# Cached memory keys of a decoder step: turned in 32x32 squares on VectorE in place of whole transposes on TensorE

## The chip, the cores and the metric

The kernel runs on one core of a Trainium2 chip. The metric is the device time of one execution in microseconds: the median of three timed runs is 949.08, between 947.50 and 950.35. A profile of one execution stands beside them. All numbers are in float32 at the inputs and outputs.

## The reference, cut to what matters

The program is one layer of a decoder for two groups with the same weights: a prompt of 512 rows and a sample group of 8 sequences with 4 new rows each. The layer has a mixer (an mLSTM and a differential attention), a cross-attention into 256 memory tokens, and a gated feed-forward with a short convolution. The change touches the cross-attention of the sample group alone:

```python
# h: (8, 4, 1024) normalised rows; cache_mem_k, cache_mem_v: (8, 256 tokens, 4 heads, 256)
q = (h @ w_mq).reshape(B, T, 4, 256)
s = einsum('bqhd,bkhd->bhqk', q, mk) * 256 ** -0.5
p = softmax(s, axis=-1)
o = einsum('bhqk,bkhd->bqhd', p, mv).reshape(B, T, 1024)
return o @ w_mo
```

Each of the 8 sequences has its own keys and values, 1 MB of each, which no other sequence shares: 8.4 MB of keys and 8.4 MB of values are read for 32 query rows.

## The kernel before, in words

Matmuls contract over the 128 partitions, so the scores need keys with the feature on the partition, and memory holds them with the token there. Products with weights split each operand into a rounded part and a rest (three matmuls per product); products of the sample rows are plain float32 matmuls with 32 columns of weights, put on the four 32-column groups of the array in turn. Such a plain float32 product stands in the trace as two records, a transpose or a product of rounded parts as one.

A planner orders the instructions of every engine when the program is built, by the place in the program, raised priorities (`tc.high_priority`) and a simulated clock; each engine then runs its list strictly in that order. `burst(t)` makes an instruction follow `t` at once. A tile is taken from a pool with a fixed number of buffers and waits until the buffer's last user has finished.

The stage around the change runs like this.

1. The query projection `gemmB(hqT, [ev_q(m) ...])`: eight column tiles of w_mq, of which m = 0 to 3 come first and m = 4 to 7 in a loop of 16 steps. `ev_q` scales each result; the sample rows' part goes to `qs` (feature on the partition, 32 query rows).
2. `mk_load(i)` reads one of 16 key tiles (sequence b, token half c): 128 tokens on the partitions, 4 KB each, into one of six `stage` buffers. `mk_turn(i)` makes eight 128x128 transposes on TensorE, and ScalarE and VectorE copy the results out of PSUM into a `kT` tile (one of the four weight slots, one tile for each sequence). Tiles 0 to 7 are turned inside the projection's loop, 8 to 15 between the first and the second four sequences' scores.
3. `mk_scores(b)`: eight products of 256 columns for each sequence (4 heads x 2 feature halves). All 32 query rows are multiplied with the keys of one sequence, and only this sequence's four rows count. `sample_exp` takes maximum and exponential for each sequence.
4. `sample_softmax` (shared with the decode attention of the mixer) mixes the eight sequences' rows through `csz` into one tile of 128 rows (sequence, head, row) x 256 tokens, which is transposed twice and spread into `az`.
5. `mv_load` and `mv_out` do the value products: `VORD` is their order, the first six tiles in stage buffers, the others in the four weight slots and one large buffer.

Between these, `next(prompt)` puts one step of the prompt group's cross-attention (scores, softmax, transposes, value products, in a pipeline four deep) into TensorE's stream. All loads of this stage are issued on SP's queue in order, with the weights of w_mo behind them.

Of the kernel before, what the change touches and what calls it, by code (L numbers as in the profile page):

```python
# [32 lines left out]
CONST_COLS = {}  # L33
_off = 0
for _n, _w in (("ident", 128), ("cos", 40), ("sin", 40), ("nsin", 40), ("dmask", 8), ("cm4", 4), ("cA", 1), ("cB", 1),
               ("comb", 16), ("selD", 8), ("selX", 8), ("selB", 8), ("cmask", 128), ("maskT", 128), ("maskS", 32)):
    CONST_COLS[_n] = (_off, _w)
    _off += _w
CONST_W = _off
# [38 lines left out]
def kernel(ctx: ExitStack, tc: tile.TileContext, I, O):  # L78
# [23 lines left out]
    def S(shape, dt, name):  # L102
        return sp.tile(list(shape), dt, name=name, tag="S")
# [10 lines left out]
    def at(name="at"):  # L114
        return psa.tile([P, 512], F32, name=name, tag="at")
# [11 lines left out]
    def v2(t, b):  # L127
        return t.rearrange("p (a b) -> p a b", b=b)
# [26 lines left out]
    def con(n, p=P):  # L155
        o, w = CONST_COLS[n]
        return cpk[:p, o:o + w]
# [51 lines left out]
    def stage():  # L209
        return stg.tile([P, 1024], F32, name="wst", tag="st")  # L210
# [847 lines left out]
    def sample_softmax(sall, su, coef, sel, oname, between=None):  # L1058


        cf = small(NB, "scf")
        nc.vector.reciprocal(out=cf, in_=su)
        if coef is not None:
            VTS(out=cf, in0=cf, scalar1=coef, scalar2=None, op0=MUL)
        VTT(out=cf, in0=cf, in1=sel, op=MUL)
        VTT(out=view(csz, 0, [(64, NB // 2), (48, 2), (1, 16)]),
            in0=con("comb").unsqueeze(1).unsqueeze(1).broadcast_to([P, NB // 2, 2, 16]),
            in1=cf.rearrange("p (i e) -> p i e", e=2).unsqueeze(3).broadcast_to([P, NB // 2, 2, 16]), op=MUL)
        az = S([P, 2, H, NB * NS], F32, oname + "z")
        nc.gpsimd.memset(az, 0.0)  # L1070
# [7 lines left out]
        behind = between() if between else None  # L1078
        pT = at("spt")
# [7 lines left out]
        return a, [az[:, 0], az[:, 1]]  # L1087

    def gather(name, b, g, out):
        v = nc.sync.value_load(ptab[0:1, 2 * b + g:2 * b + g + 1], min_val=0, max_val=I[name].shape[1] - 1)  # L1090
# [303 lines left out]
        split(mvN[0][:, c], mvN[1][:, c], st)  # L1394

    qs = sm.tile([P, 8, NS], F32, name="qs", tag="qz", bufs=1)
    qh, ql = [], []

    def ev_q(m):
        if m % 2 == 0:  # L1400
            qh.append(npool.tile([P, 2, 516], F32R, name="qh", tag="N"))
        if m % 4 == 0:
            ql.append(S([P, 4, SEQ], F32R, "ql"))

        def ev(i, c0, c1, ps):
            n = min(c1, SEQ) - c0
            q = qh[m // 2][:, m % 2, c0:c0 + n]
            nc.scalar.mul(out=q, in_=ps[:, :n], mul=1.0 / 16.0)
            STT(out=ql[m // 4][:, m % 4, c0:c0 + n], in0=ps[:, :n], scalar=1.0 / 16.0, in1=f32(q), op0=MUL, op1=SUB)
            if i == 1:  # L1410
                nc.scalar.mul(out=qs[:, m, :], in_=ps[:, n:n + NS], mul=1.0 / 16.0)
        return ev

    run(gemmB(hqT, [ev_q(m) for m in range(4)], half_first=True))
# [44 lines left out]
            j = 2 * (h % 2) + e  # L1459
            put(oT, h // 2, j, j + 1, 0, SEQ, po.unsqueeze(1))  # L1460

    kst, kts, vts = {}, {}, {}

    def mk_load(i):
        b, c = i // 2, i % 2
        kst[i] = stage()
        dma(out=kst[i], in_=I["cache_mem_k"][0, b, c * P:(c + 1) * P].rearrange("t h d -> t (h d)"))

    def mk_turn(i):
        b, c = i // 2, i % 2  # L1470
        if c == 0:
            kts[b] = wp.tile([P, 8, 256], F32, name="kT", tag="W")
        for q in range(2):
            ps = at("tpk")
            for j in range(4):
                t = tr(ps[:, j * P:(j + 1) * P], kst[i][:, (4 * q + j) * P:(4 * q + j + 1) * P], ident)
            (VCP if q else nc.scalar.copy)(out=kts[b][:, 4 * q:4 * q + 4, c * P:(c + 1) * P], in_=v2(ps, P))
        return t.ins

    def mk_scores(b):  # L1480
        ps = mmp("ssc")[:, :256]
        for c in range(2):
            for h in range(H):
                t = mm(ps[NS * h:NS * h + NS], lhsT=qs[:, 2 * h + c], rhs=kts[b][:, 2 * h + c, :], start=(c == 0), stop=(c == 1))
        sample_exp(sall, b, ps, nm, su)
        return t.ins

    def mv_load(b):

        if 2 < b:  # L1490
            t = wp.tile([P, 2, DM], F32, name="vt", tag="W") if b < 7 else S([P, 2, DM], F32, "vt")
            vts[b] = [t[:, 0], t[:, 1]]
        else:
            vts[b] = [stage(), stage()]
        for c in range(2):
            dma(out=vts[b][c], in_=I["cache_mem_v"][0, b, c * P:(c + 1) * P].rearrange("t h d -> t (h d)"))

    VORD = [(b, 1 - c if b in (2, 7) else c) for b in (2, 1, 0, 7, 6, 5, 4, 3) for c in range(2)]

    def mv_out(bs):  # L1500

# [7 lines left out]
    sall = S([P, NB, 256], F32, "cas")  # L1509
    nm, su = small(NB, "snm"), small(NB, "ssu")  # L1510
    prompt = pipe(8, ch_soft, lambda i: None, ch_turn, ch_out)

    for i in range(6):
        mk_load(i)
    for i, _ in enumerate(gemmB(hqT, [ev_q(m) for m in range(4, 8)])):
        if i % 4 == 3:
            for j in (i // 2 - 1, i // 2):
                mk_turn(j)
                mk_load(j + 6)

    next(prompt)
    for b in range(4):
        t = mk_scores(b)
    with tc.issue_after(t):
        for j in range(8, 16):
            t = mk_turn(j)
            if j + 6 < 2 * NB:
                mk_load(j + 6)
            if j == 11:
                next(prompt)  # L1530
    for b in range(3):
        mv_load(b)
    next(prompt)
    with tc.issue_after(t):
        for b in range(4, NB):
            t = mk_scores(b)
    for b in range(3, NB):
        mv_load(b)
    next(prompt)
    with tc.high_priority():  # L1540
        _, az = sample_softmax(sall, su, None, con("selX"), "ca")
    for _ in range(NMID):
        next(prompt, None)
    pso = mmp("pso")[:, :256]
# [347 lines left out]
def _constants():  # L1892
# [28 lines left out]
    put("selD", ((r % 16 // TS)[:, None] == np.arange(NB)[None, :] % 4).astype(np.float32))  # L1921
    put("selB", ((r // 16)[:, None] == np.arange(NB)[None, :]).astype(np.float32))
    put("selX", ((r % NS // TS)[:, None] == np.arange(NB)[None, :]).astype(np.float32))
    return {"consts": c}


# [20 lines left out]
```

## Time and profile before

| | |
|---|---|
| timed runs, median (lowest to highest) | 949.08 us (947.50 to 950.35) |
| the profiled execution, first to last instruction | 947.0 us, its own time; no other is given for it |
| TensorE busy | 927.3 us, 98% of the span |
| VectorE, ScalarE, GpSimd busy | 601.1, 388.5, 195.9 us |
| bytes moved | 130.27 MB, mean 138 GB/s |
| TensorE's granted clock, mean | 0.995 |

TensorE's matmuls are pipelined: a record begins before the one ahead has ended, so a sum of durations counts overlap twice. What a group costs in the stream is the time from its first start to the start of what follows. PE is the matmul side of TensorE, PEld its weight loads, DVE is VectorE, ACT ScalarE, POOL GpSimd and SP the queue that issues DMAs (SPq in the rows).

### The profile page before, as it was taken

Reading aid. Unit: us, or ns where it says so; the run is one execution under the profiler, and the core shown is the slowest. Engines: PE = TensorE matmul, PEld = TensorE weight load, DVE = VectorE, ACT = ScalarE, POOL = GpSimd, SP = SyncE. Lnnn points to the kernel's source line nnn. Section 1 sums busy time; section 2 is a strip of 40 time slices with the busy share of each in tenths; the row PEclk is TensorE's granted clock in tenths of the full one; section 3 lists DMA queues with packets and bytes.
Section 4 is the critical chain, followed back from the end, with each engine's and each line's share of the span. In section 5 each row is a group of like instructions: output and inputs, shape, how many; then the busy total and the mean of one; then the engine's idle time right before and its main releaser. Section 6 shows DMA issues by size and latency. Waiting matters only on the chain. (4 is left out here: it accounts for less than half of the span.)

```text
span 947.0 us, 17080 instructions
## 1 busy us (share of the span) xinstructions
PE 927.3 (98%) x6612; PEld 808.2 (85%) x6612; DVE 601.1 (63%) x1128; ACT 388.5 (41%) x750; POOL 195.9 (21%) x384
## 2 busy tenths in 40 slices
PE   8999999999999999999999999999999999999995
PEld 5899787889866778998777899989988998999974
DVE  6745145565887448735654778637757775676767
ACT  5655233344676457625544433322212222222232
POOL 6611000025432215300000554001110110110114
PEclk9999999999999999999999999999999999999998
DMA  8960023344870429946944732062043313512023
GB/s 273 301 197 7 1 89 137 89 123 139 270 265 7 165 97 340 297 155 211 358 167 135 209 122 80 26 179 67 17 133 108 94 27 96 149 49 90 24 92 117
DMA packets 120673, 130.27 MB, mean 138 GB/s; under 512 B 8567, under 2 KB 86232, under 8 KB 120592
## 3 DMA queue, kind: packets, MB, share of 16 engines
q1 hardware_dynamic: 114408, 125.69, 42.1%
q10 hardware_dynamic: 6184, 3.48, 1.2%
q8 instruction: 52, 0.85, 0.4%
q14 instruction: 29, 0.24, 0.1%
HBM read 112.22 MB, written 16.93 MB: 136 GB/s over the span
## 5 line engine op out<-in xcount | busy, mean ns | idle before, releaser
L485 PE MATMUL mm<-fT,wslot 128*128 128x256 f32 x1872 | 235.9, 288 | 0.0
L485 PEld LDWEIGHTS mm<-fT,wslot 128*128 128x128 f32 x1872 | 234.4, 188 | 1.8 <-issue 0.8
L146 ACT CAST wslot<-wst 128x1024 fp32r<-128x1024 f32 x125 | 130.8, 1050 | 251.3 <-issue 71.7
L147 DVE TENSOR_TENSOR wslot<-wst,wslot 128x1024 fp32r<-128x1024 f32 x125 | 155.1, 1245 | 81.3 <-ACT wslot L146 80.8
L1758 PE MATMUL mm<-wslot,act 128*128 128x512 f32 (+1 forms) x180 | 70.2, 391 | 0.0
L1759 PE MATMUL mm<-wslot,act 128*128 128x512 f32 (+1 forms) x180 | 70.0, 392 | 0.0
L1757 PE MATMUL mm<-wslot,act 128*128 128x512 f32 (+1 forms) x180 | 69.3, 387 | 0.0
L1663 POOL COPY cvo<-u 128x2 f32<-128x2 f32 x43 | 10.5, 243 | 203.6 <-DVE u L1661 193.5
L411 PE MATMUL mm<-wslot,hT 128*128 128x512 f32 x128 | 51.3, 402 | 0.0
L485 PE MATMUL mm<-hT,wslot 128*128 128x256 f32 (+1 forms) x384 | 51.0, 289 | 0.0
L413 PE MATMUL mm<-wslot,hT 128*128 128x512 f32 x128 | 51.0, 399 | 0.0
L412 PE MATMUL mm<-wslot,hT 128*128 128x512 f32 x128 | 50.8, 397 | 0.0
L1658 DVE TENSOR_TENSOR u<-mm,rsb 128x256 f32<-128x256 f32 x43 | 18.1, 424 | 50.0 <-PE mm L485 50.0
L485 PEld LDWEIGHTS mm<-hT,wslot 128*128 128x128 f32 x384 | 49.2, 188 | 0.5 <-issue 0.2
L1757 PEld LDWEIGHTS mm<-wslot,act 128*128 128x128 f32 x180 | 34.3, 191 | 8.0 <-issue 0.8
L1759 PEld LDWEIGHTS mm<-wslot,act 128*128 128x128 f32 x180 | 33.8, 188 | 7.3 <-issue 0.4
L1758 PEld LDWEIGHTS mm<-wslot,act 128*128 128x128 f32 x180 | 33.8, 188 | 7.2
L1675 ACT ACTIVATE c<-c 128x560 f32<-128x560 f32 x21 | 14.1, 672 | 56.7 <-DVE c L1669 56.7
L1669 DVE SCALAR_TENSOR_TENSOR c<-u,cvT,c 128x560 f32<-128x560 f32 x43 | 34.3, 797 | 0.9
L1668 DVE SCALAR_TENSOR_TENSOR c<-u,cvT,c 128x560 f32<-128x560 f32 x43 | 34.1, 793 | 0.2
L1770 DVE TENSOR_TENSOR yp<-mm,yp 128x512 f32<-128x512 f32 (+1 forms) x41 | 27.2, 673 | 5.2 <-PE mm L1759 5.1
L413 PEld LDWEIGHTS mm<-wslot,hT 128*128 128x128 f32 x128 | 24.1, 188 | 5.0
(476 smaller groups left out, 1850.8 us busy)
## 6 DMA issues: line engine op xcount, KB each, us to landing
wst<-in_w_up_dram SPq DMA_DIRECT2D x42, 512.0 KB
wst<-in_w_in_dram SPq DMA_DIRECT2D x28, 512.0 KB
wst<-in_w_down_dram SPq DMA_DIRECT2D x20, 512.0 KB
wst<-in_cache_mem_k_dram SPq DMA_DIRECT2D x16, 512.0 KB
vt<-in_cache_mem_v_dram SPq DMA_DIRECT2D x10, 512.0 KB
wst<-in_w_mk_dram SPq DMA_DIRECT2D x8, 512.0 KB
xb<-in_x_prompt_dram SPq DMA_DIRECT2D x8, 512.0 KB
wst<-in_cache_dk_dram SPq DMA_DIRECT2D x16, 256.0 KB
```

Of the source, the lines that this page charges most:

```text
L146: nc.scalar.copy(out=hi, in_=src)
L147: (eng or nc.vector).tensor_tensor(out=lo, in0=src, in1=f32(hi), op=SUB)
L411: mm(ps[b], lhsT=xt.hi(k, c0, c0 + n), rhs=s[:, 0, kk, :], start=(k == 0), stop=False)
L412: mm(ps[b], lhsT=xt.hi(k, c0, c0 + n), rhs=s[:, 1, kk, :], start=False, stop=False)
L413: return mm(ps[b], lhsT=xt.lo(k, c0, c0 + n), rhs=s[:, 0, kk, :], start=False, stop=(k == nk - 1))
L485: mm(ps[i], lhsT=s[:, l, k, :], rhs=x(k, c0, c1), start=(k == 0 and j == 0), stop=(k == 7 and j == 2))
L1668: STT(out=c, in0=u[:, 1:EXT - 1], scalar=w[1], in1=c, op0=MUL, op1=ADD)
L1669: STT(out=c, in0=u[:, 0:EXT - 2], scalar=w[0], in1=c, op0=MUL, op1=ADD)
L1757: mm(ps, lhsT=t[:, 0, c0:c0 + P], rhs=s[:, 0, i % 2, cs], start=st, stop=False)
L1758: mm(ps, lhsT=t[:, 0, c0:c0 + P], rhs=s[:, 1, i % 2, cs], start=False, stop=False)
L1759: return mm(ps, lhsT=t[:, 1, c0:c0 + P], rhs=s[:, 0, i % 2, cs], start=False, stop=en)
L1770: VTT(out=y, in0=ps, in1=y, op=ADD)
```

## The change

The keys of all four heads of 32 tokens are read by one DMA for each head: head h goes to partitions 32h to 32h+31, with the token within 32 on the partition and four blocks of 32 tokens behind each other. `nc.vector.transpose` then turns every 32x32 square of the tile in place, so that partition 32h + f holds feature f of head h for a block of 32 features. The queries lie in `qx`, zero but for a block-diagonal: row 32h + f of block j, and one column for each sequence, head and row. One product then contracts 32 features of all four heads at once, for a pair of sequences' 32 query columns; eight blocks of features fall on four column groups, twice each. `mk_sum` adds the four groups and picks a sequence's 16 columns by a matrix of zeros and ones (`selE`), which gives the tile of 128 rows directly, and one softmax works on it. Keys and values of a sequence use the same buffers (`two`, `home`), and the order of sequences is 0, 2, 4, 6, 1, 3, 5, 7. `attend_T` is the end of `sample_softmax`, taken out; the decode attention still uses both.

```diff
+    qx = cst.tile([P, 8, NB, 4 * TS], F32, name="qx", tag="xs")
+    nc.gpsimd.memset(qx, 0.0)
+    def mq_spread(h):
+        for j in range(4):
+            nc.gpsimd.tensor_copy(out=view(qx[NS * h:NS * h + NS, j, :, TS * h:TS * h + TS], 0, [(512, 2), (16, NB), (1, TS)]),
+                                  in_=qs[NS * j:NS * j + NS, 2 * h:2 * h + 2, :].rearrange("p c (n t) -> p c n t", t=TS))
...
                 nc.scalar.mul(out=qs[:, m, :], in_=ps[:, n:n + NS], mul=1.0 / 16.0)
+                if m % 2 == 1:
+                    mq_spread(m // 2)
...
+    SEQS, HOMES = (0, 2, 4, 6, 1, 3, 5, 7), (0, 1, 2, 7, 3, 4, 5, 6)
+    home = dict(zip(SEQS, HOMES))
+    def two(i):
+        if i < 3:
+            return [stage(), stage()]
+        t = wp.tile([P, 2, DM], F32, name="kvt", tag="W") if i < 7 else S([P, 2, DM], F32, "kvt")
+        return [t[:, 0], t[:, 1]]
+    def mk_load(b):
+        kst[b] = two(home[b])
         for c in range(2):
             for h in range(H):
-                t = mm(ps[NS * h:NS * h + NS], lhsT=qs[:, 2 * h + c], rhs=kts[b][:, 2 * h + c, :], start=(c == 0), stop=(c == 1))
-        sample_exp(sall, b, ps, nm, su)
+                dma(out=v2(kst[b][c][NS * h:NS * h + NS], 256),
+                    in_=I["cache_mem_k"][0, b, c * P:(c + 1) * P, h].rearrange("(k t) d -> t k d", t=NS))
+    def mk_turn(b):
+        for t in kst[b]:
+            nc.vector.transpose(out=t, in_=t)
+    def mk_scores(bs):
+        t = None
+        for b in bs:
+            ps = mmp("ssc")[:, :256]
+            for c in range(2):
+                kv = kst[b][c].rearrange("p (k j t) -> p k j t", j=8, t=NS)
+                for j in range(8):
+                    g = NS * (j % 4)
+                    with burst(t):
+                        t = mm(v2(ps[g:g + NS, c * P:c * P + P], NS), lhsT=qx[:, j, b // 2 * 2:b // 2 * 2 + 2].rearrange("p n r -> p (n r)"),
+                               rhs=kv[:, :, j, :], start=(j < 4), stop=(j >= 4)).ins
+            nc.scalar.copy(out=sc[:, b], in_=ps)
+        return t
+    def mk_sum(last):
+        t = None
+        for b in SEQS:
+            i = NS * (b // 2)
+            with tc.issue_after(last) if t is None else burst(t):
+                t = mm(pS[i:i + NS], lhsT=con("selE")[:, NS * (b % 2):NS * (b % 2) + NS], rhs=sc[:, b], start=(b % 2 == 0),
+                       stop=(b % 2 == 1)).ins
+    def mem_softmax():
+        nm, su = small(NB, "snm")[:, 0:1], small(NB, "ssu")[:, 0:1]
+        VRED(out=nm, in_=pS, axis=AX.X, op=MAX, negate=True)
+        a = Z("spc")[:, :256]
+        ACT(out=a, in_=pS, func=AF.Exp, bias=nm, accum_out=su)
+        nc.vector.reciprocal(out=su, in_=su)
+        VTS(out=a, in0=a, scalar1=su, scalar2=None, op0=MUL)
+        return attend_T(a, "ca")
...
-    VORD = [(b, 1 - c if b in (2, 7) else c) for b in (2, 1, 0, 7, 6, 5, 4, 3) for c in range(2)]
+    VORD = [(SEQS[k], 1 - c if k in (2, 3) else c) for k in (2, 1, 0, 3, 7, 6, 5, 4) for c in range(2)]
...
+    pS = at("pS")[:, :256]
+    for k in range(4):
+        mk_load(SEQS[k])
     for i, _ in enumerate(gemmB(hqT, [ev_q(m) for m in range(4, 8)])):
+        if i % 4 == 1:
+            mk_turn(SEQS[i // 4])
         if i % 4 == 3:
-            for j in (i // 2 - 1, i // 2):
-                mk_turn(j)
-                mk_load(j + 6)
+            mk_load(SEQS[4 + i // 4])
     next(prompt)
...
     next(prompt)
+    sc = S([P, NB, 256], F32, "sc")
+    mk_scores(SEQS[:4])
+    for k in range(3):
+        mv_load(SEQS[k])
+    mv_load(SEQS[3])
+    for k in range(4, 8):
+        mk_turn(SEQS[k])
     next(prompt)
+    t = mk_scores(SEQS[4:])
+    for k in range(4, 8):
+        mv_load(SEQS[k])
+    next(prompt)
+    mk_sum(t)
     with tc.high_priority():
-        _, az = sample_softmax(sall, su, None, con("selX"), "ca")
+        az = mem_softmax()
```

## Rows read from the trace of the kernel before

**Rows 1.** The page's first lines: busy us (share of the span) and records

```profile
span 947.0 us, 17080 instructions
PE 927.3 (98%) x6612; PEld 808.2 (85%) x6612; DVE 601.1 (63%) x1128; ACT 388.5 (41%) x750; POOL 195.9 (21%) x384
```

**Rows 2.** Windows: length, then busy PE, PEld, DVE, ACT, POOL, clock, DMA share, GB/s

```profile
404.00:436.00 32.00, 32.00 (x265) 32.00 (x264) 9.50 (x19) 9.34 (x24) 1.81 (x1) 1.00 0.46 144
436.00:456.00 20.00, 19.94 (x233) 15.44 (x231) 13.37 (x30) 11.43 (x36) 0.00 (x0) 1.00 0.85 291
...
450.00:470.00 20.00, 19.94 (x186) 15.86 (x185) 13.83 (x36) 12.38 (x44) 0.00 (x0) 1.00 1.02 393
```

**Rows 3.** TensorE's timeline, cross-attention stage: start us, length us, line, operation, count

```profile
414.39 0.60 PE L1476 MATMUL tpk<-cpk,wst 128*128 128x128 f32 x4
414.74 4.00 PE L485 MATMUL mm<-hqT,wslot 128*128 128x256 f32 x30
...
434.10 1.47 PE L1476 MATMUL tpk<-cpk,wst 128*128 128x128 f32 x12
435.32 0.48 PE L1427 MATMUL sca<-mkT,qh 128*128 128x256 f32 x2
...
436.92 1.05 PE L1484 MATMUL ssc<-kT,qs 128*32 128x256 f32 x10
437.90 0.66 PE L1476 MATMUL tpk<-cpk,wst 128*128 128x128 f32 x4
438.49 3.22 PE L1484 MATMUL ssc<-kT,qs 128*32 128x256 f32 x54
441.64 1.53 PE L1476 MATMUL tpk<-cpk,wst 128*128 128x128 f32 x12
442.93 0.48 PE L1427 MATMUL sca<-mkT,qh 128*128 128x256 f32 x2
...
447.61 5.09 PE L1476 MATMUL tpk<-cpk,wst 128*128 128x128 f32 x40
452.63 3.66 PE L1484 MATMUL ssc<-kT,qs 128*32 128x256 f32 x64
...
470.48 2.80 PE L1506 MATMUL pso<-wst,caz 128*32 128x256 f32 x48
...
475.55 4.52 PE L1506 MATMUL pso<-vt,caz 128*32 128x256 f32 x80
```

**Rows 4.** TensorE's timeline: value products of the decode attention, and the softmax mixing

```profile
286.57 1.95 PE L1337 MATMUL ops<-vt,daz 128*32 128x128 f32 x64
288.46 0.94 PE L1281 MATMUL oda<-dvN,aT 128*128 128x128 f32 x6
...
460.52 1.07 PE L1075 MATMUL spa<-cas,csz 128*32 128x256 f32 x16
```

**Rows 5.** Groups by line on VectorE, 404 to 486: count, busy us, mean ns, idle before

```profile
L1477 DVE COPY kT<-tpk 128x512 f32<-128x512 f32 x16 | 11.0, 686 | 9.0 <-PE tpk L1476 9.0
```

**Rows 6.** Instructions by tile, whole trace: count, ns least/median/most, first and last start

```profile
L318 DVE TENSOR_SCALAR hN<-xb,rs x5: 731/753/756, 22.0 to 48.2; 128x1024 f32<-128x1024 f32 x4, 32x1024 f32<-32x1024 f32 x1
...
L147 DVE TENSOR_TENSOR wslot<-wst,wslot x125: 1187/1220/2319, 31.4 to 916.3; 128x1024 fp32r<-128x1024 f32 x125
...
L1221 POOL COPY kT<-dkT x8: 191/198/199, 222.3 to 260.8; 128x16 f32<-128x16 f32 x8
...
L254 SPq DMA_DIRECT2D wst<-in_w_up_dram x44: 367/378/1684, 512.0 to 853.2; - x44
...
L1141 SPq DMA_DIRECT2D xb<-in_x_sample_dram x1: 337/337/337, 289.8 to 289.8; - x1
```

**Rows 7.** Timeline of SP's queue, waits between issues included: start us, length us

```profile
393.36 29.74 SPq L1467 DMA_DIRECT2D wst<-in_cache_mem_k_dram  x10
```

**Rows 8.** Bytes moved from 290.5 to 292.5, in 40 columns of 0.05 us

```profile
GB/s 0 0 0 0 0 328 410 328 246 328 246 82 0 0 0 246 328 82 0 0 0 0 0 0 0 0 0 0 0 0 0 0 0 0 0 0 0 0 0 0
```

More of the change, by code (lines that the diff above doesn't have):

```diff
@@ L35 @@
 for _n, _w in (("ident", 128), ("cos", 40), ("sin", 40), ("nsin", 40), ("dmask", 8), ("cm4", 4), ("cA", 1), ("cB", 1),
-               ("comb", 16), ("selD", 8), ("selX", 8), ("selB", 8), ("cmask", 128), ("maskT", 128), ("maskS", 32)):
+               ("comb", 16), ("selD", 8), ("selX", 8), ("selB", 8), ("selE", 64), ("cmask", 128), ("maskT", 128), ("maskS", 32)):
     CONST_COLS[_n] = (_off, _w)
@@ L1068, in sample_softmax @@
             in1=cf.rearrange("p (i e) -> p i e", e=2).unsqueeze(3).broadcast_to([P, NB // 2, 2, 16]), op=MUL)
-        az = S([P, 2, H, NB * NS], F32, oname + "z")
-        nc.gpsimd.memset(az, 0.0)
         w = sall.shape[2]
@@ L1078, in sample_softmax, with attend_T @@
         behind = between() if between else None
+        return a, attend_T(a, oname, behind)
+    def attend_T(a, oname, behind=None):
+        az = S([P, 2, H, NB * NS], F32, oname + "z")
+        nc.gpsimd.memset(az, 0.0)
         pT = at("spt")
@@ L1086, in sample_softmax @@
                 nc.scalar.copy(out=view(az, g * 1024 + h * 256, [(36, NB), (1, TS)]), in_=src[:, h])
-        return a, [az[:, 0], az[:, 1]]
+        return [az[:, 0], az[:, 1]]
     def gather(name, b, g, out):
@@ L1460, in ch_out @@
             put(oT, h // 2, j, j + 1, 0, SEQ, po.unsqueeze(1))
[L1462 to L1478, printed above, removed]
@@ L1480, in mk_scores @@
-    def mk_scores(b):
-        ps = mmp("ssc")[:, :256]
+    kst, vts = {}, {}
+    SEQS, HOMES = (0, 2, 4, 6, 1, 3, 5, 7), (0, 1, 2, 7, 3, 4, 5, 6)
[7 more added lines that the diff above has]
+        kst[b] = two(home[b])
         for c in range(2):
             for h in range(H):
-                t = mm(ps[NS * h:NS * h + NS], lhsT=qs[:, 2 * h + c], rhs=kts[b][:, 2 * h + c, :], start=(c == 0), stop=(c == 1))
-        sample_exp(sall, b, ps, nm, su)
-        return t.ins
@@ L1488, in mv_load @@
-    def mv_load(b):
[L1490 to L1494, printed above, removed]
+                dma(out=v2(kst[b][c][NS * h:NS * h + NS], 256),
[3 more added lines that the diff above has]
+            nc.vector.transpose(out=t, in_=t)
@@ L1495, in mv_load @@
+    def mv_load(b):
+        vts[b] = two(home[b])
         for c in range(2):
             dma(out=vts[b][c], in_=I["cache_mem_v"][0, b, c * P:(c + 1) * P].rearrange("t h d -> t (h d)"))
-    VORD = [(b, 1 - c if b in (2, 7) else c) for b in (2, 1, 0, 7, 6, 5, 4, 3) for c in range(2)]
+    VORD = [(SEQS[k], 1 - c if k in (2, 3) else c) for k in (2, 1, 0, 3, 7, 6, 5, 4) for c in range(2)]
     def mv_out(bs):
@@ L1507, in mv_out @@
                            rhs=vts[b][c][:, 256 * h:256 * h + 256], start=((b, c) == VORD[0]), stop=((b, c) == VORD[-1])).ins
-    sall = S([P, NB, 256], F32, "cas")
-    nm, su = small(NB, "snm"), small(NB, "ssu")
     prompt = pipe(8, ch_soft, lambda i: None, ch_turn, ch_out)
-    for i in range(6):
-        mk_load(i)
+    pS = at("pS")[:, :256]
+    for k in range(4):
+        mk_load(SEQS[k])
     for i, _ in enumerate(gemmB(hqT, [ev_q(m) for m in range(4, 8)])):
+        if i % 4 == 1:
+            mk_turn(SEQS[i // 4])
         if i % 4 == 3:
-            for j in (i // 2 - 1, i // 2):
-                mk_turn(j)
-                mk_load(j + 6)
+            mk_load(SEQS[4 + i // 4])
     next(prompt)
[L1522 to L1532, printed above, removed]
-    next(prompt)
[L1534 to L1538, printed above, removed]
-    next(prompt)
+    next(prompt)
+    sc = S([P, NB, 256], F32, "sc")
[5 more added lines that the diff above has]
+        mk_turn(SEQS[k])
+    next(prompt)
+    t = mk_scores(SEQS[4:])
[3 more added lines that the diff above has]
+    mk_sum(t)
     with tc.high_priority():
-        _, az = sample_softmax(sall, su, None, con("selX"), "ca")
+        az = mem_softmax()
     for _ in range(NMID):
@@ L1923, in _constants @@
     put("selX", ((r % NS // TS)[:, None] == np.arange(NB)[None, :]).astype(np.float32))
+    put("selE", np.concatenate([((r % NS)[:, None] == s[None, :]) & (s[None, :] // 16 == e) for e in range(2)], 1))
     return {"consts": c}
```

## The prediction

> **What bounds the kernel now.** I read the page's first lines, then the windows by stage, then TensorE's timeline of the stage that the change touches. TensorE is busy for 98% of the span [rows 1]; in the cross-attention stage it is busy 32.00 of 32 us and 19.94 of 20 us, at a granted clock of 1.00 (the 2.4 GHz level), while VectorE, ScalarE and GpSimd have half of their time free or more [rows 2]. So an instruction that leaves TensorE's stream gives back its own time, as long as the rest of the stream still finds its data. The other engines and the transfers matter only as possible new waits. The timeline is read from start to next start, since matmul ends overlap.
>
> **Turning squares leaves TensorE: -14.0 us.** The 128 transposes of `mk_turn` stand in twelve groups between matmuls. A group of 12 lasts 1.22 to 1.29 us (434.10 to 435.32, 441.64 to 442.93), and there are five; a group of 4 lasts 0.35 (414.39 to 414.74), once 0.59 (437.90 to 438.49), and there are five; one of 40 lasts 5.02 (447.61 to 452.63); one of 8 lies between and is taken at the same 0.1 us each [rows 3]. Sum: 5 x 1.24 + 4 x 0.35 + 0.59 + 0.8 + 5.0 = 14.0 us. All lie on TensorE's unbroken stream.
>
> **Scores: 0 (from -0.2 to +7.7).** Before, 64 products of 256 columns run as 128 records: 0.98 us for 10 (436.92 to 437.90), 3.15 for 54 (438.49 to 441.64) and 3.66 for 64, 7.7 us in all [rows 3]. After, 8 sequences x 2 tiles x 8 blocks = 128 products of 128 columns on four 32-column groups in turn, 256 records. The decode attention's value product has this very shape: 64 records from 286.57 to 288.46, 29.5 ns each [rows 4]. 256 x 29.5 ns = 7.6 us. What differs is that the moving operand now comes in four runs of 32 elements; no row shows that, and I bound it by the old pace per record (57 ns, +7.7 for 256 records started at half the columns) and take the nearest row, so 0. Each sequence is multiplied by a pair's 32 query columns, half of them unused, which costs no more than the 32-column shape of that row.
>
> **Selector sums: 0.** `mk_sum` is 8 products of 32x256, as the eight that mix `csz` in before: 16 records, 1.07 us [rows 4]. They change places.
>
> **Softmax: off the path, 0.** Eight maxima on VectorE and eight exponentials on ScalarE become one of each plus eight plain copies. After the sums, the chain maximum, exponential, reciprocal, scale, two transposes, eight copies stands before the value products. Three steps of the prompt pipeline are put between, as before; between 460.52 (sums) and 470.48 (value products) [rows 3, 4] TensorE had 10 us of that work, and the chain is a handful of operations of at most 128x256, half the size of the 686 ns copy in [rows 5]. If this cover failed, its cost would be under 3 us.
>
> **Queries spread on GpSimd: +0.3 (0 to 1.5).** Sixteen small copies and a memset. The nearest row is a 128x16 GpSimd copy of 198 ns [rows 6]. Only the last four wait for the last query tile; 0.8 us after it, while two prompt steps (1.6 us each: 435.32 to 436.92 [rows 3]) run on TensorE first. GpSimd was almost idle here (1.81 us of 32 [rows 2]); a copy of 0.5 us would give the upper end.
>
> **Squares on VectorE: hidden.** Added: 16 in-place turns of 128x1024. No row shows a 32x32 turn; VectorE's rows of that size between two on-chip tiles run from 753 ns (one source) to 1220 (two sources), longest 2319 [rows 6]. I take 1.2. Removed: 16 evictions of 686 ns [rows 5], 11 us, and seven of the maxima; added 19 us. VectorE was busy 9.50 of 32 and 13.37 of 20 us [rows 2], so it fits by sum; what counts is the last one, below.
> The Trainium skill, "VectorE: DVE Perf Modes", section "The three transpose paths", gives 311 ns for a VectorE turn of 128x128 in bf16; as an estimate from that page eight of these are 2.5 us for one tile, beyond the longest row of 2319 ns. No row here shows a turn of four-byte elements; by it two turns end 2.6 us later than I take, which the spare time below would just cover, or the sum is up to 3 us higher.
>
> **When the last keys are ready: +1.0 (0 to 8.6).** On the clock of before, less what was removed: the projection ends at 434.10 - 4.7 (three groups of 12 and three of 4 ahead of it) = 429.4. Two prompt steps, 3.2, bring the first four scores to 432.6, and they take 3.85; a prompt step of 2.0 follows; the second four start at 438.4, and the last sequence is needed 2.9 later, at 441.3. Its buffer is a weight slot that comes free at 429.4. Loading it is eight DMAs, each issued in 0.37 to 0.38 us as the weights' are [rows 6], so 3 us of issue on SP's queue.
> The only row like these DMAs is the sample rows' load: 32 partitions, 128 KB, issued at 289.8 [rows 6], its bytes moving from 290.75 to 291.40, in 13 of the 0.05 us columns [rows 8]: 0.65 us, or 0.8 with the edges. Eight one after the other: 429.4 + 1.0 + 5.2 = 435.6; two turns of 1.2 us, the first of which starts earlier: 437 to 438. So 3 us are spare.
> The queue as a whole is tighter. Key loads begin at 393.4 as in before [rows 7] and run freely from some 397.5: I allow 4 us for the weight loads still ahead of them. 64 DMAs x 0.37 (issue bound) = 24 us; 64 x 0.65 = 42 us, to 439.1, plus a turn of 1.2 = 440.3: still before 441.3. At 0.8: 51 us, 448.7 and 449.9, a wait of 8.6 us. Consecutive DMAs go to different partitions and several are open at once, so I expect less than 0.65 each. I charge 1.0 us for disorder: four copies of SP's work at the head of the queue, VectorE in order with three prompt softmaxes between the turns.
> The Trainium skill, "SBUF — State Buffer", section "Door 1: The DMA port swizzle", says that 32 partitions reach only half of the 16 ports, so that such a transfer has half the bandwidth. As an estimate from that page it is 0.6 us for 128 KB, and the 0.65 us of the row agrees with it for a DMA alone. It speaks against this change: by it the key loads take 38 us and the spare 3 us shrink to almost nothing, yet the sum stays.
>
> **Values behind the keys: 0.** 8.4 MB at 393 GB/s (the rate of 450 to 470 [rows 2]) take 21 us, from 436 to 457. The value products, 14 us earlier than 470.48 and 475.55 [rows 3], need the first six tiles at 456.5 and the rest from 461.5. The buffers are the keys' own, free after each group of scores. Late next would be the output weights queued behind them, which are first used after all value products.
>
> **Sum.** -14.0 + 0 + 0.3 + 1.0 = -12.7. The profiled execution spans 947.0 us [rows 1] and becomes 934.3. The median of the three timed runs, 949.08, is 2.1 above that span; carried over: 936.4. Its own range is 933.5 to 939.
>
> **Rivals.**
> *Keys or turns are late, a smaller gain:* 939 to 946. The second four scores stand in TensorE's order before later prompt work, so a late key stops the whole stream. For it: four times as many DMAs, each to a quarter of the partitions, and at 0.65 us each only 1 us is spare. With 0.8 it is 936.4 - 1.0 + 8.6 = 944. With turns of 2.32 us instead of 1.2 the last two end 2.2 us later, behind prompt softmaxes: 2 to 3 us, 938 to 939.5. Against it: several DMAs move at once, and 512 KB loads in this stretch reach 291 GB/s [rows 2].
> *Key loads become the bound, slower than before:* If a 32-partition DMA holds the queue for d, TensorE waits 64 x d - 42.6 us (397.5 to 440.1, when the last must land). The gain of 13.7 without disorder is used up at d = 0.88 us. At 1.0 us the wait is 21.4: 949.1 - 13.7 + 21.4 = 956.8. For it: from issue to last byte the row has 1.6 us (289.8 to 291.4), so at least two must be open at all times. Against: the bytes themselves took 0.65.
> *Score products run at the pace of their weight loads:* each record has its own load of 32 columns; should the 256 records pace at over 85 ns instead of 29.5, the 14 us are gone. At twice the old record, 115 ns, 936.4 + 21.9 = 958. Against: the same shape at 29.5 ns [rows 4].
> *No change* needs d near 0.88 and is a narrow place between.
>
> **How the numbers follow.** A measurement of this kernel tells about 0.3% (2.8 us) from no change, so faster is under 946.2 and slower over 951.9. Forecast (933.5 to 939): 0.67. Late keys or turns (939 to 946): 0.17. No change: 0.06. Slower: 0.10, of it 0.07 the loads and 0.03 the products. Faster 0.84, same 0.06, slower 0.10. The range, 933 to 946, leaves out the last two cases and a little on the low side.
>
> **What will show it.** Right: no transposes of keys on TensorE; 256 score records at about 30 ns; the projection's last four tiles end some 4.7 us earlier and the value products start 13 to 14 earlier; TensorE still at 98%. Wrong: an idle stretch on TensorE before the second four scores, ended by VectorE (turn late) or behind it a key DMA; score records near 57 ns; turns over 2 us; SP's queue busy with key loads past 440; a wait of the value products for their transfers. A gain over 15 us would mean that something else was lifted that I don't see.

## The result, and the profile after

Forecast: 936.4 us. Measured: 954.27 us median (950.42 to 956.37), beside 949.23 for the kernel before on the same chip; ratio 1.0044, 95% interval 1.0028 to 1.0061 (the two medians by themselves give 1.0053). So the change costs 0.3 to 0.6% where a gain of 1.3% was forecast. The profiled execution took 950.42 us and spans 948.6; before spanned 947.0 [rows 1]. It is the fastest of four executions: the other three took 953.96 to 956.37, at a mean granted clock of 0.986 to 0.989 against its 0.990, and no trace shows where they lose the further 3.5 to 6 us.

The page's first lines of the changed kernel:

```profile
span 948.6 us, 17140 instructions
PE 918.3 (97%) x6612; PEld 800.8 (84%) x6612; DVE 606.2 (64%) x1120; ACT 377.7 (40%) x727; POOL 202.6 (21%) x401
```

TensorE is busy for 9.0 us less than in [rows 1], and the span is 1.6 us longer: the time has become waiting and a lower clock. (`conv_mid_heads`, below, has the same work on TensorE at a clock of 1.00 throughout this stage and is busy for 913.4 us. So, as an estimate, nearly 5 of the 918.3 us here are work that ran slower.) The windows (columns as in [rows 2]) say where, first of the changed kernel, then the last two of before:

```profile
403.00:420.00 17.00, 13.23 (x92) 12.82 (x91) 13.24 (x15) 2.37 (x7) 1.82 (x8) 0.90 0.82 183
420.00:436.00 16.00, 16.00 (x131) 16.00 (x131) 8.79 (x11) 2.40 (x9) 0.92 (x4) 1.00 1.07 202
436.00:452.00 16.00, 12.84 (x292) 11.20 (x290) 10.70 (x22) 7.75 (x26) 2.74 (x5) 1.00 0.90 311
452.00:470.00 18.00, 17.69 (x161) 14.28 (x165) 11.24 (x30) 9.86 (x38) 0.00 (x0) 1.00 0.74 260
470.00:485.00 15.00, 10.52 (x112) 6.92 (x100) 7.77 (x12) 7.16 (x14) 0.00 (x0) 0.92 0.91 324
485.00:500.00 15.00, 15.00 (x57) 11.79 (x57) 4.75 (x18) 2.05 (x5) 0.00 (x0) 0.85 0.11 35
```
```profile
470.00:485.00 15.00, 15.00 (x183) 10.88 (x182) 11.20 (x20) 9.82 (x22) 0.00 (x0) 1.00 0.74 264
485.00:500.00 15.00, 15.00 (x66) 11.93 (x65) 4.76 (x18) 2.05 (x5) 0.00 (x0) 1.00 0.11 35
```

Three holes in a stream that was whole before: 3.8 us idle from 403 to 420, 3.2 from 436 to 452, 4.5 from 470 to 485. In and after the first and the third the granted clock is under 1.00 (0.90, 0.92, 0.85: part of the stretch at the lower, 1.2 GHz level); in before it was 1.00 in all these stretches. TensorE's waits from 403 to 490 (total us, times, longest):

```profile
PE mm L485 <- ACT qs L1423: 3.8, 2, 3.4
PE ost L1595 <- ACT oS L1592: 3.4, 1, 3.4
PE ssc L1510 <- POOL qx L1408: 2.4, 1, 2.4
PE cpo L1471 <- ACT pT L146: 1.1, 1, 1.1
PE pS L1521 <- issue: 1.0, 1, 1.0
```

TensorE's timeline (compare [rows 3]), then the output projection's first record in before, to set beside the last line:

```profile
438.71 3.57 PE L1510 MATMUL ssc<-wst,qx 128*32 128x128 f32 x95 [2.42 <-POOL qx L1408]
...
445.22 3.70 PE L1510 MATMUL ssc<-kvt,qx 128*32 128x128 f32 x128
...
464.89 2.80 PE L1548 MATMUL pso<-wst,caz 128*32 128x256 f32 x48
...
469.63 4.52 PE L1548 MATMUL pso<-kvt,caz 128*32 128x256 f32 x80
...
481.40 0.44 PE L1595 MATMUL ost<-cpk,oS 128*128 128x128 f32 x2 [3.38 <-ACT oS L1592]
...
484.98 0.71 PE L411 MATMUL mm<-wslot,oT 128*128 128x512 f32 x1
```
```profile
485.18 0.39 PE L411 MATMUL mm<-wslot,oT 128*128 128x512 f32 x1
```

The transposes are gone. The second 128 score records take 3.6 us, as costed; the first 128 take 4.5 (438.71 to 443.20), because their first weight loads follow the four copies into `qx` one by one. The value products begin 5.6 us earlier than in before (470.48), and the output projection 0.2: what was left of the gain is lost between these two points.

**The first hole is VectorE's order.** Its timeline:

```profile
396.33 0.42 DVE L1421 SCALAR_TENSOR_TENSOR ql<-mm,qh 128x256 fp32r<-128x256 f32 x1
403.45 1.25 DVE L1498 STREAM_TRANSPOSE wst<-wst 128x1024 f32<-128x1024 f32 x1 [6.71 <-DMA wst<-in_cache_mem_k_dram]
...
407.14 1.20 DVE L1498 STREAM_TRANSPOSE kvt<-kvt 128x1024 f32<-128x1024 f32 x1
408.26 1.18 DVE L147 TENSOR_TENSOR wslot<-wst,wslot 128x1024 fp32r<-128x1024 f32 x1
409.37 0.41 DVE L1421 SCALAR_TENSOR_TENSOR ql<-mm,qh 128x256 fp32r<-128x256 f32 x1
```

A turn took 1.25 us (1.2 assumed). VectorE stands 6.7 us at the first one until its keys land. Behind it in the written order are a weight split and an eviction (L147, L1421). ScalarE's `qs` waits for that eviction, and the projection waits for `qs`. Most of the second hole (2.4 us) has the same root: the last query eviction (437.43) stands behind a turn that starts at 436.26, after a wait of 0.76 us for its keys, and the four `qx` copies (1.10 us) stand behind it.

**The third hole is SyncE's queue.** Issues, start and length, in before and then in the changed kernel:

```profile
423.16 0.42 SPq L1570 DMA_DIRECT2D cr<-in_state_conv_dram  x1
...
441.37 0.25 SPq L1572 DMA_DIRECT2D cr<-in_b_dw_dram  x1
...
471.18 3.42 SPq L231 DMA_DIRECT2D wst<-in_w_mo_dram  x6
```
```profile
440.24 0.83 SPq L1538 DMA_DIRECT2D wst<-in_cache_mem_v_dram  x2
...
445.14 0.27 SPq L1608 DMA_DIRECT2D cr<-in_w_dw_dram  x1
446.43 0.25 SPq L1609 DMA_DIRECT2D cr<-in_b_dw_dram  x1
...
469.31 0.25 SPq L1609 DMA_DIRECT2D cr<-in_b_dw_dram  x1
469.60 1.25 SPq L1145 DMA_DIRECT2D xb<-x_d  x3
470.94 3.10 SPq L231 DMA_DIRECT2D wst<-in_w_mo_dram  x6
```

`cr` is the state and weights of a later convolution: 24 small DMAs. Before, all of them were issued from 423.2 to 441.4, between key loads. Now 20 of them stand between and behind the values, many some 1.27 us apart: eleven waited, up to 1.4 us each, for the landing of an earlier value load. One group of the waits of SP's queue, and ScalarE's timeline:

```profile
SPq L1607 <- DMA kvt<-in_cache_mem_v_dram: 2.8, 3, 1.0
```
```profile
477.49 2.24 ACT L146 CAST wslot<-wst 128x1024 fp32r<-128x1024 f32 x2 [5.95 <-PE cpo L1471]
...
480.98 0.37 ACT L1592 COPY oS<-pso 128x256 f32<-128x256 f32 x1
```

Behind the small loads come `xb` and only then the output weights, at 470.94 (471.18 before), although the value products that free their buffers are 5.6 us earlier. ScalarE casts these weights from 477.49 on in its written order, ahead of the copy `oS` (480.98) for which TensorE waits.

### The profile page after: what moved, and what is told of

Read it like the earlier page. It is cut to its first block, busy times and chain, and to the rows that moved or that the text cites. A ratio compares the mean times of both kernels' runs of the same rounds, so it can differ in the third digit from the quotient of the medians.

```text
span 948.6 us, 17140 instructions
## 1 busy us (share of the span) xinstructions
PE 918.3 (97%) x6612; PEld 800.8 (84%) x6612; DVE 606.2 (64%) x1120; ACT 377.7 (40%) x727; POOL 202.6 (21%) x401
## 5 line engine op out<-in xcount | busy, mean ns | idle before, releaser
L147 DVE TENSOR_TENSOR wslot<-wst,wslot 128x1024 fp32r<-128x1024 f32 x125 | 155.2, 1246 | 83.3 <-ACT wslot L146 82.8
L485 PE MATMUL mm<-hqT,wslot 128*128 128x256 f32 x192 | 26.2, 299 | 3.8 <-ACT qs L1423 3.8
```

The costliest lines, as they stand in the source:

```text
L147: (eng or nc.vector).tensor_tensor(out=lo, in0=src, in1=f32(hi), op=SUB)
L485: mm(ps[i], lhsT=s[:, l, k, :], rhs=x(k, c0, c1), start=(k == 0 and j == 0), stop=(k == 7 and j == 2))
```

## Experiments

Theory: two causes that have nothing to do with the turns' own cost, (a) key loads onto 32 partitions are slow, and engines wait in written order behind the turns, (b) the small loads hold SyncE's queue. Rivals: the score shape, the spread queries, the turns themselves. Each edit is to the changed kernel, `before_32` apart; each ratio is to the kernel before, timed beside it. In `heads_128`, `conv_mid_heads` and `before_32` the keys lie in wrong places, and `no_turns` leaves the turn out: these four measure a cause and are no kernels to use. The kernel before with its small loads moved was not run; its TensorE had no hole in this stage that this could close.

**Loads onto 128 partitions** (`heads_128`)
```
-  for h: dma(out=v2(kst[b][c][NS*h:NS*h+NS], 256), in_=...[.., h].rearrange("(k t) d -> t k d", t=NS))
+  for h: dma(out=kst[b][c][:, 256*h:256*h+256], in_=...[.., h])
```


> The changed kernel with the same 64 key DMAs of 128 KB in 1 KB pieces, but each puts one head's 256 features of 128 tokens on 128 partitions instead of 32 tokens x 4 blocks on 32 partitions; the scores are of wrongly placed keys. Theory (the 32 partitions halve the rate, and the turns queued ahead of the evictions wait for the keys): the 1 KB pieces fall from 80 ns to about 46, key loads move at 300 GB/s or more, the waits of 3.8 and 2.4 us on TensorE before the first scores go, 938 to 946 us. Rival (four times as many issues and pieces on SP's queue are the trouble, not the partitions): no change, 951 to 956 us.


948.16 us, ratio 0.9980 (0.9966 to 0.9994): 6 us less than the changed kernel, but 2 us above the theory's range. The early waits shrink to 1.4 and 0.2 us. VectorE still stands 4.4 us at its first turn, but that is nearly short enough for TensorE not to notice. The output weights still come late against the value products, at 467.85, and TensorE waits 4.2 us ahead of the output projection.

```profile
PE mm L485 <- ACT qs L1423: 1.4, 1, 1.4
```

Packets and bytes in a stretch of key loads, with their share of 16 engines, of the changed kernel (412 to 424) and then of this one (408 to 418):

```profile
q1 hardware_dynamic: 2525, 2.30, 91.6%
```
```profile
q1 hardware_dynamic: 2140, 1.95, 64.5%
```

2.30 MB are 17.5 loads of 131 kB in 0.916 x 12 us: 0.63 us of all engines for one. Onto 128 partitions: 14.9 loads in 0.645 x 10 us, 0.43 us. So (a) is real; it is not the whole. The edit changes two things about a load, the partitions that it writes and the order in which it reads the rows of keys, and no run separates them fully. `head_order`, below, changes only which partitions neighbouring loads write, and its loads get faster too, so the partitions are at least a part of it.

**Turns behind evictions** (`late_turns`) and **heads in another order** (`head_order`)
```
-  if i % 4 == 1: mk_turn(SEQS[i // 4])
+  if i % 4 == 3: with tc.issue_after(<last ql eviction>): mk_turn(SEQS[i // 4])
---
-  for h in range(H):
+  for h in (0, 2, 1, 3):
```


> The changed kernel with the turns of the first four sequences each put behind the eviction of the projection's next column tile on VectorE; loads untouched. Theory (rate and order): the 3.8 us before the projection's second loop tile go with their slow clock, but the keys, values and output weights arrive as late as before, so TensorE waits later instead: 948 to 954 us. Rival (only VectorE's order is wrong): the gain of 14 us comes back for the most part, 938 to 944 us.


954.29 us, ratio 1.0061 (1.0042 to 1.0079): no gain, as expected. The projection's wait is now one of 4.4 us, until 427.3. VectorE's timeline shows why: a turn of the second four, which the edit left free, now stands ahead of two evictions.

```profile
422.88 1.25 DVE L1498 STREAM_TRANSPOSE kvt<-kvt 128x1024 f32<-128x1024 f32 x1 [8.74 <-DMA kvt<-in_cache_mem_k_dram]
...
426.86 0.72 DVE L1421 SCALAR_TENSOR_TENSOR ql<-mm,qh 128x256 fp32r<-128x256 f32 x2
```


> The changed kernel with the four heads of a tile loaded in the order 0, 2, 1, 3, so that neighbouring DMAs write to different halves of the partitions. Theory: if two engines on one port drift apart by one DMA they stop sharing it and the pieces fall towards 46 ns: 944 to 952 us; if they stay in step nothing changes, 952 to 956. Rival (number of DMAs): no change.


950.84 us, ratio 1.0014 (1.0003 to 1.0025). From 412 to 424, 2.38 MB took 87% of the engines, 0.57 us a load where the changed kernel had 0.63, and the early waits stay (4.5 us for `qs`; that for `qx` falls to 1.1). Whether the faster loads are all of the 3 us that it gains on the changed kernel is not settled.

**The kernel before with the change's loads** (`before_32`)
```
-  dma(out=kst[i], in_=... "t h d -> t (h d)")
+  for h: dma(out=v2(kst[i][NS*h:NS*h+NS], 256), in_=...[.., h].rearrange("(k t) d -> t k d", t=NS))
```


> The kernel before with its key tiles loaded by 64 DMAs of 32 partitions as in the change, all else as before (TensorE transposes, so the scores are of wrongly placed keys). Theory: the slower loads make the transposes wait and push values and output weights back: 952 to 962 us. Rival (loads are harmless by themselves, the turns on VectorE are what waits): no change, 948 to 950 us.


950.24 us, ratio 1.0007 (0.9998 to 1.0017): the theory's 952 to 962 is a miss. The same kind of loads costs nothing here: TensorE's first transpose of keys starts only at 410.18, where VectorE in the changed kernel stood ready for its first turn at 396.7 and got the keys at 403.4. So the cost is that of late keys and an early place in an engine's order together. Its window from 403 to 436 and the first transposes:

```profile
403.00:436.00 33.00, 33.00 (x274) 33.00 (x273) 9.88 (x19) 9.53 (x24) 1.81 (x1) 1.00 0.66 162
```
```profile
410.18 1.47 PE L1478 MATMUL tpk<-cpk,wst 128*128 128x128 f32 x12
```

**Blocks of tokens onto 128 partitions** (`blocks_128`, `conv_mid_blocks`)
```
+  for k in range(4): dma(out=kst[b][c][:, 256*k:256*k+256], in_=<heads, 32 tokens, features> of block k)
```


> The changed kernel with the same 64 key loads of 128 KB in 1 KB pieces, cut otherwise: one load per chunk and block of 32 tokens, all four heads, onto 128 partitions (before: one head, four blocks, 32 partitions). Result unchanged. Theory (a load onto 32 partitions takes 0.6 us instead of 0.35, the first turns wait, and the projection behind them): the waits of TensorE between 403 and 440 shrink from 3.8 + 2.4 us to under 2 in all; time 945 to 950, as the loads onto 128 partitions in natural order gave (948.2). Rival (the natural order of tokens mattered, not the partitions): 953 to 955, as the changed kernel.


1002.74 us, ratio 1.0581 (1.0551 to 1.0611), far from both. The window from 420 to 436 shows the transfers at a steady 90 GB/s and a share of 0.27, as if only some four of 16 engines carried them (which, the view does not say):

```profile
420.00:436.00 16.00, 8.40 (x48) 8.37 (x48) 6.62 (x7) 0.95 (x4) 0.92 (x4) 0.60 0.27 89
```


> Both at once: key loads onto 128 partitions and the small loads ahead of the values. Result unchanged. Theory (the two causes together hid the gain of the change): output weights issued at 462 to 465, output projection starts 6 to 9 us earlier than 485.0 less the start of the second projection loop, time 938 to 943. Rival (a third wait, such as the values' own transfers, takes the place): 945 to 948, output weights still held.


997.71 us, ratio 1.0506 (1.0478 to 1.0535), with the same 89 GB/s and share of 0.27. It says nothing of (b), and as `blocks_128` failed, its question (partitions or the order of rows) stays open as said above.

**Small loads ahead of the values** (`conv_mid`)
```
   mk_load(SEQS[4 + i // 4])
+  conv_in(cr, ...) for two of its eight parts, behind each of these four loads
```


> The changed kernel with its 24 small loads of the convolution state issued among the later key loads, ahead of the values, instead of between and behind the values. Theory (they and the waits for a free place hold the output weights on SyncE's queue until 470.9): the output weights are issued at 465 to 468, the idle time of TensorE ahead of the output projection falls from 3.4 us to under 1, time 949 to 952; the early waits stay. Rival (the stage buffers or the transfers themselves hold the output weights): 953 to 956, weights still at 470 to 471.


944.37 us, ratio 0.9946 (0.9925 to 0.9967): more than expected. The weights come at 469.17, not at 465 to 468; that part missed, since in this execution the keys' last loads went out at 442 to 447. But the value products (466.39), the weights and `oS` are now in step, the third hole is gone with its low clock, and the first is left (4.1 us of waits for `qs`):

```profile
403.00:420.00 17.00, 12.91 (x91) 12.49 (x90) 11.49 (x12) 2.97 (x7) 0.91 (x4) 0.89 0.74 180
...
470.00:485.00 15.00, 15.00 (x138) 10.71 (x137) 9.24 (x20) 8.74 (x20) 0.00 (x0) 1.00 1.04 371
485.00:500.00 15.00, 15.00 (x77) 11.35 (x76) 6.46 (x14) 2.96 (x4) 0.00 (x0) 1.00 0.33 108
```

**Turns left out** (`no_turns`): `mk_turn` does nothing.


> The changed kernel with its 16 turns of the keys left out (scores of unturned keys); loads as they are, onto 32 partitions. Theory (VectorE, in its strict order, stands at a turn that waits for its keys, and the weights' splits and the evictions stand behind it): with no turn there the waits of 0.41 and 3.4 us in the projection vanish; the scores of the first four sequences now wait for keys or spread queries by up to 3 us; time 948 to 952. Rival (the transfers themselves starve the projection's weights): the wait in the projection stays at 3 to 4 us, time 953 to 955.


948.73 us, ratio 0.9995 (0.9985 to 1.0005). With the same slow loads there is no wait before 436: not the transfers starved the projection but VectorE's stand at the turns.

```profile
403.00:436.00 33.00, 33.00 (x365) 32.66 (x364) 9.37 (x20) 8.75 (x29) 4.59 (x13) 1.00 0.96 201
```

Later, 2.8 us of waits for value loads and 4.9 us ahead of the output projection remain.

**Both causes taken away** (`conv_mid_heads`): `conv_mid` with the loads of `heads_128`.


> The changed kernel with both causes taken away: the small loads of the convolution state ahead of the values (that alone gave 944.4), and key loads of the same 128 KB onto 128 partitions in the natural order of tokens (the scores are of wrongly placed keys). Theory (two causes, the late keys still cost the first of the two about 5 us): no wait over 1 us in the projection, granted clock 1.00 from 403 to 436, time 937 to 941. Rival (the late keys cost nothing once the output weights come in time): 943 to 946.


936.55 us, ratio 0.9868 (0.9840 to 0.9897); the forecast was 936.4, a ratio of 0.9866. The rival (943 to 946) is out. TensorE's waits from 395 to 540, then its timeline:

```profile
PE cpt L1459 <- DVE cp L1450: 0.7, 1, 0.7
PE pso L1547 <- DMA kvt<-in_cache_mem_v_dram: 0.4, 1, 0.4
```
```profile
431.75 2.83 PE L1509 MATMUL ssc<-wst,qx 128*32 128x128 f32 x96
...
438.53 3.97 PE L1509 MATMUL ssc<-kvt,qx 128*32 128x128 f32 x128
...
457.00 2.80 PE L1547 MATMUL pso<-wst,caz 128*32 128x256 f32 x48
461.73 1.07 PE L1547 MATMUL pso<-kvt,caz 128*32 128x256 f32 x16
```
The forecast had these four at 432.6, 438.4, 456.5 and 461.5. So the rest of its sum holds within about 1 us, and the two causes account for the miss: together they are worth 16.7 us (1.0044 to 0.9868) of the 16.9 between forecast and result. That the time agrees to 0.2 us is luck, as the interval is some 2.7 us to either side. VectorE still stands 3.6 us at its first turn here, and TensorE does not wait for it.

**Two queues for the keys** (`conv_mid_act`, `conv_mid_pool`): `conv_mid`, with the third and fourth heads' loads issued by `nc.scalar` or `nc.gpsimd`.


> Small loads ahead of the values, and key loads as in the change, onto 32 partitions each, but the loads of the third and fourth heads issued by ScalarE on its own queue, so that loads onto different partitions can run side by side. Result unchanged. Theory (each load is slow for its own 32 partitions, the transfers of two queues run side by side): key loads done by about 425 instead of 448, time 937 to 942. Rival 1 (the packets share one rate): keys as late, 943 to 946. Rival 2 (ScalarE, in its order, stands at issues that wait, and the evictions stand behind it): 946 to 955.


943.95 us, ratio 0.9942 (0.9920 to 0.9964): rival 1, with some of rival 2 (2.6 us of wait for a split on ScalarE). The keys' last loads go out by 444.6. From 409 to 433 one takes 0.52 us of all engines (4.47 MB, 73.5% of 24 us, a few small loads among them); `conv_mid`, with one queue, has 0.58 in the same window (4.31 MB, 78.9%). So side by side they share the rate for the most part.


> As the one before, with the third and fourth heads' loads issued by GpSimd on its queue. Result unchanged. Theory (side by side, and GpSimd has little else to do): 937 to 942. Rival (GpSimd's issues are slow, or the spreading of the queries stands behind them): 944 to 955.


951.86 us, ratio 1.0020 (1.0005 to 1.0036): the rival. GpSimd's loads land 4.4 to 4.7 us after their issue, VectorE stands 13.3 us at its first turn, and the projection waits 9.1 us in one piece for a split behind it.

**Can an order of the turns do it at half rate?** All with the change's loads.


> Small loads ahead of the values, key loads as in the change on one queue, and the turns of the first four sequences put on VectorE behind the projection's last eviction so far. Result unchanged. Theory (with half-rate loads the wait only moves later, as it did when that was done alone, 954.3): 942 to 946. Rival (once the output weights come in time, the moved wait is covered): 937 to 941.


942.84 us, ratio 0.9930 (0.9907 to 0.9952), the theory's range; TensorE waits 3.4 us for `ql` behind a turn of the second four, as in `late_turns`. So those were ordered too:
```
+  with tc.issue_after(<last ql eviction>):
       for k in range(4, 8): mk_turn(SEQS[k])
```


> Small loads ahead of the values, key loads as in the change (half rate), and every turn kept behind evictions on VectorE: those of the first four sequences each behind the last eviction emitted so far, those of the second four behind the last eviction of the projection (in the kernel without that, at 942.8, a turn of the second four stood at 414 to 421.6 for its keys with two evictions behind it, and TensorE waited 3.4 us). Theory (the second part is VectorE's order, not the rate): no wait of TensorE over 1 us between 403 and 436, time 936 to 940. Rival (half-rate loads cost the second part in any order): 941 to 944, the wait moved to the scores of the second four.


946.93 us, ratio 0.9979 (0.9968 to 0.9989): both theory and rival missed. No wait in the projection, first scores at 431.3; but seven turns in a row then stand ahead of the prompt's softmax, and two more behind them wait for their keys (0.75 and 2.19 us). VectorE's timeline and TensorE's one wait:

```profile
429.51 7.99 DVE L1498 STREAM_TRANSPOSE kvt<-kvt 128x1024 f32<-128x1024 f32 x7
```
```profile
PE cpt L1459 <- DVE cp L1450: 11.9, 1, 11.9
```


> As the one before, with the turns of the first four sequences a further group of the projection later (the fourth of them behind its last eviction). Theory: 936 to 940 as well; if the earlier placing still has a turn waiting, this one is the lower. Rival (the turns now pile up behind the projection, 10 of 1.2 us, ahead of the softmax of the prompt): 941 to 945, TensorE waits for turned keys at the second scores.


948.50 us, ratio 0.9987 (0.9975 to 0.9999): slower than even its rival said, and for a like reason: one wait of 10.2 us, but at the prompt's transposes and not at the second scores.


> The changed kernel with that order of the turns alone, the small loads where the change had them (between and behind the values). Theory (two separate causes): the waits between 403 and 440 fall under 1.5 us in all but the output weights still come at 466 to 471, as with the turns left out (948.7); time 947 to 950. Rival (the two are one, late keys push the small loads back): 938 to 943.


946.96 us, ratio 0.9977 (0.9961 to 0.9992), the same as `conv_mid_last`, which differs in the small loads alone. The rival (938 to 943) is out. But the theory's weights at 466 to 471 did not come true either: they go out at 464.47, since the same wait (7.7 us here) gives the queue time again, and 1.6 us ahead of the output projection is left. So cause (b) has no fixed price: it shows where the stage is otherwise short. And small loads moved ahead of the values are not free: they push the keys back, and the wait is 11.9 us in `conv_mid_last`.

Last, the second four's turns woven between the softmax steps (`issue_after` on the `cp` of one), with the small loads ahead of the last projection weights or as in `conv_mid`:


> Half-rate key loads as in the change. The small loads stand ahead of the last projection weights (from about 380, where SyncE's queue has idle time); the turns of the first four sequences behind evictions; those of the second four behind the first and second softmax step of the prompt, so that no softmax step of these stands behind a turn that waits. Theory (VectorE's order is the cause): no wait of TensorE over 2 us between 403 and 485, time 936 to 940. Rival (rate: the last sequence's keys land at 437 to 441 and the second scores wait for them): a wait of 3 to 6 us at the second scores, time 941 to 945.


942.39 us, ratio 0.9928 (0.9904 to 0.9952): the rival's time, but not its wait. The waits at the second scores sum to 2.7 us in five pieces of at most 0.7. But a wait of 3.1 us has come up earlier, in the projection, with a clock of 0.91 from 385 to 403. The small loads now hold SyncE's queue from 380.1 to 391.4, so the prompt's memory values (`mv_d`) and the projection's weights go out at 391.4 and 392.3 (385.4 and 385.8 in the changed kernel). VectorE stands 8.7 us at the split of those values, with the projection's evictions behind it: the first cause again, with another load.


> As the one before, with the last sequence's turn behind the third softmax step and the second scores one step of the prompt's pipeline later. Theory: 936 to 940; if the one before waits at the second scores, this one does not. Rival (later scores make the memory's softmax late, and the values wait for it): a wait at the value products, 941 to 946.


943.46 us, ratio 0.9949 (0.9929 to 0.9969): the wait at the second scores does not go (2.5 us for a turn, 0.5 for a copy), and the 3.1 stay.


> As woven_early2, with the small loads among the later key loads, where they take some 8 us of SyncE's issue time from the last keys. Theory: 937 to 941, close to woven_early2. Rival (the last keys land at 445 and something waits): 942 to 946.


946.61 us, ratio 0.9971 (0.9959 to 0.9983), a little over its rival's range: no wait in the projection, 2.5 us at the second scores as before, and the values, behind late keys, hold TensorE 3.7 us at the value products.

So with the half-rate loads each order tried pays somewhere: at the projection, the softmax, the second scores or the values. Whether some order pays nothing is open. Of the kernels that compute the reference, `woven_early` and `conv_mid_late` have the lowest ratios and beat the kernel before by 0.5 to 1.0% and the changed one by about 1.1%. `conv_mid`, `conv_mid_act` and `woven_early2` cannot be told apart from them by the intervals. None of these reaches the forecast 936.4.

## Why the prediction was wrong, step by step

- *Turning squares leaves TensorE, -14.0; scores 0; selector sums 0:* right, as `conv_mid_heads` shows (TensorE busy for 13.9 us less than before; the old scores' 7.7 us are 7.8 by their rows); in the changed kernel the first scores were some 0.9 us slower, as said above. The spread queries took 1.10 us for the last four copies where 0.8 was reckoned. They were late because their eviction stood behind a turn: in `heads_128` TensorE's wait for them is 0.2 us, and the term of 0.3 fits.
- *Squares on VectorE, hidden:* the size was right (1.25 us for 1.2). The step failed at "what counts is the last one". The first one counts: it stood 6.7 us, and the projection's splits and evictions behind it. The sum's 1.0 for disorder named prompt softmaxes between the turns; nothing asked what of the projection is queued behind a waiting turn. `no_turns` (ratio 0.9995 against 1.0044, about 4.6 us) and `heads_128` (0.9980, about 6) price it; with cause (b) gone it is 7.4 us (`conv_mid` to `conv_mid_heads`). The Trainium skill, "VectorE: DVE Perf Modes", section "The three transpose paths", led to an estimate of 2.5 us a tile; the trace disagrees for these four-byte squares, with 1.245 in the median of 16.
- *When the last keys are ready, +1.0:* the rate was right, 0.63 us a load for 0.65. The last key load was issued by 438.2 and its turn at 442.26 no longer waited for it; landing at 439.1 was reckoned, and no wait stood at the second scores. "I expect less than 0.65 each" hardly came true. The Trainium skill, "SBUF — State Buffer", section "Door 1: The DMA port swizzle", gives 32 partitions half of the ports and, for large transfers, half of the bandwidth; the runs show 0.63 against 0.43 us, two thirds. The prediction's remark that by that page the spare 3 us shrink does not follow: 64 loads at 0.6 us are 38 us, less than the 42 that it had reckoned.
- *Values behind the keys, 0; "late next would be the output weights queued behind them":* the place was named and priced at nothing. This step failed too. The 24 small loads, which had gone out among the key loads on the same queue, and `xb` were not counted; most of the small loads came behind the first values and held the output weights until 470.94. `conv_mid` prices them: 1.0044 to 0.9946, about 9 us with the clock that they cost in this order of the stage (nothing between `turns_last` and `conv_mid_last`).
- Of the rivals, *late keys or turns* named the right engines at the wrong end of the stage; *key loads become the bound* had the right sign, but its 0.88 us a load was not reached, so that the time fell where this rival had it is luck.

## What to carry to other kernels

When an operation moves to an engine that runs in written order and its data come by DMA, price the first instance as well as the last: list what stands behind it and who waits for that. When a stretch gets shorter on the main engine, list every DMA that the queue issued in its slack, small ones too; they do not shrink with it, and the next stage's weights can stand behind them.

## What the runs showed of the hardware

- A turn of 128x1024 four-byte elements in 32x32 squares took VectorE 1.20 to 1.25 us, in place.
- Key loads of 131 kB in 1 kB pieces took 0.63 us of all engines onto 32 partitions (0.57 with the heads in the order 0, 2, 1, 3) and 0.43 onto 128, where the rows were also read in another order; from two queues onto different partitions 0.52, against 0.58 from one in the same window.
- A load whose source has four rows of heads outermost, onto 128 partitions, moved at 90 GB/s with a share of 0.27 (`blocks_128`); loads of the same size in `heads_128` moved 195 GB/s (1.95 MB in 10 us) with a share of 0.645.
- Small loads behind value loads of 512 KB on the same queue often came some 1.27 us apart, though each is issued in 0.3 us: eleven of them waited for a value load to land (changed kernel). In `before`, among key loads, they mostly went out 0.3 to 0.5 us apart.
